# Routed experts of a decoder block: a third buffer of output rows, rows gathered four blocks ahead, and the down products of small blocks in four parts

## The chip, the core and the metric

The kernel runs on one core of a Trainium2 chip. The metric is device time in microseconds (us), from the first to the last instruction with the launch around it; smaller is better. The core has five engines that run their own instruction streams and wait for each other by semaphores: TensorE (PE in the profile, PEld for its weight loads), VectorE (DVE), ScalarE (ACT), GpSimd (POOL) and SyncE (SP). Sixteen DMA engines move data between the large memory (HBM) and the on-chip memories; POOL and SP both issue transfers to them.

## What is computed

The kernel is one layer of a decoder: a mixing part (a state-space branch and a sparse attention branch) and a channel part, a mixture of 64 experts for 1024 tokens of width 1024. Only the end of the channel part is touched. Cut to that, the reference is:

```
scores = sigmoid(xt @ w_router)                    # 1024 tokens x 64 experts
top_e  = the 8 best experts of each token (limited to 4 of 8 groups)
w      = scores[top_e] / sum * 2.5
# tokens sorted by expert, padded to blocks; for each block of one expert e:
rows = xt[tok]                                     # gather
hid  = silu(rows @ w_gate[e]) * (rows @ w_up[e])   # 1024 -> 256
out  = (hid @ w_down[e]) * wt[:, None]             # 256 -> 1024
routed = zeros.at[buf_tok].add(out)                # scatter with add
x = x + gate_f * (routed + shared)
```

All arithmetic is in float32. The output rows of a block are added to rows of the output that other blocks have added to as well, since a token has eight experts.

## The kernel before, in words

The mixing part, the router and the shared expert run first and take a little over half of the time; nothing in them changes. Then `moe()` (line 2099) walks the 64 experts, ordered by how many tokens they have. A planned number of slots for an expert (`QUOTA`, line 29) is cut into blocks of at most 128 slots: 32 experts have one block of 88 to 128 slots, the others a first block of 128 and then one or two blocks of 8 to 64. That makes 98 blocks: 64 of more than 64 slots, 16 of 48 or 64, and 18 of 8 to 32.

For block b the steps are: `gather(b)` (line 1853) fetches its token rows from HBM into one of three buffers `xg`, with an indirect DMA that POOL issues; `xpose(b)` (line 2131) transposes them on PE; `gu(b)` (line 2155) makes the gate and up products; `act(b)` the nonlinearity; `ht(b)` (line 2180) transposes the hidden rows; `dn(b)` (line 2200) makes the down products into a bank of PSUM, `o`; `put(b)` (line 2212) scales them into one of two buffers `ot` and issues the scatter with add to the output, again an indirect DMA from POOL. `put` writes `ot[b % 2]`, so it waits until the scatter of block b-2 has landed. All scatters write the same tensor, so the scatter of block b waits for the landing of the scatter of block b-1 as well.

Blocks of at most 64 slots use the array in parts side by side: a weight load of 32 or 64 columns leaves room beside it, and matmuls whose outputs lie at other partitions of PSUM go there. `gu` does so in four parts (32 columns) or two (64). `dn` uses two parts for all of them, with 512 columns of `w_down` each, at partitions 0 and 64.

The order is written out by hand at lines 2234 to 2273. In turn b of the loop stand, in this order: `gu(b)`; `gather(b + 3)`; `put(b - 2)`; two thirds of the splits of the next expert's weights (`units`, an ACT cast at line 2090 and a DVE subtraction at line 2091, eight of each per expert); `ht(b - 1)`; `act(b)`; `xpose(b + 2)`; `dn(b - 1)`; the rest of the splits; after an expert's last block, the loads of the weights three experts on (`w_load`, SP, three transfers of 1 MB); and one or two steps of background work (`bg`): picking the last tokens of the long lists (lines 1868 and 1869), `merge` (line 1871), which turns the lists into the row numbers that the gathers use, and tables for experts with more tokens than slots. Before the first gather of an expert with a long list (block 7) all the steps up to `merge` must have been issued.

On POOL the instructions of the loop are therefore: gather, scatter, gather, scatter, and so on, each in its turn.

Of the kernel before, what the change touches and what calls it, by code (L numbers as in the profile page):

```python
# [13 lines left out]
I32 = mybir.dt.int32  # L14
AF = mybir.ActivationFunctionType
OP = mybir.AluOpType
# [6 lines left out]
D = 1024  # L23
# [98 lines left out]
class Kernel:  # L122
# [1976 lines left out]
    def moe(self):  # L2099
        nc, I, fp, rp = self.nc, self.I, self.fp, self.rp  # L2100
        v = nc.vector
        mm = nc.tensor.matmul
        W, order = self.W, self.order
        r4 = self.r4
        r3, gates = self.r3, self.gt

        c = 3 * (D + 64)
        self.spare, self.nov = r3[:64, c:c + 640], r3[:1, c + 640:c + 641].bitcast(I32)
        hT = self.qp.tile([P, 2, 2, P], F32, name="hT", tag="qb")
        xhs = [self.qp.tile([P, 4, 280], F32R, name="xh", tag="wraw", bufs=2) for _ in range(2)]  # L2110
        xhs = [x.rearrange("p k n -> p (k n)")[:, :D].rearrange("p (k n) -> p k n", k=KT) for x in xhs]
        ots = [r4[:, i * D:(i + 1) * D] for i in range(2)]
        self.keysF = r4[:64, 2 * D:3 * D]

        xss = [r4[:, 2 * D + 512 * i:2 * D + 512 * i + 512] for i in range(2)]
        nc.gpsimd.memset(r4[:, 2 * D:3 * D], 0.0)
        hids = self.hids = [r4[:, 3 * D + 256 * i:3 * D + 256 * i + 256] for i in range(2)]
        self.ov = r4[:1, 3 * D + 512:4 * D].bitcast(I32)
        wts, self.cols = [gates[:, i:i + 1] for i in range(6)], gates[:64, 8:24]
        gf = self.gf = self.r_gf  # L2120
        depth, nr = sum(QUOTA[0]), [sum(len(x) > q for x in QUOTA) for q in range(3)]
        r0, _ = self.first_ranks()
        bg = self.take(self.taken, depth) + [lambda: self.merge(depth, [(0, 0, r0), (1, 0, nr[1]), (2, 0, nr[2])])]
        tables = self.overflow_tables()
        bg, left = bg + tables, len(tables)
        blocks, B = self.blocks, self.B
        nb = len(blocks)
        def units(e):
            return [lambda k=k: self.gu_part(e, k, v) for k in range(len(W[e]["gu"]), KT)]
# [70 lines left out]
        def dn(b):  # L2200

            s = B[b]
            n, w, st = s["n"], W[s["e"]]["dn"], s["hst"]
            if n > 64:
                s["o"] = [self.ps("o", "mm")[:n] for _ in range(2)]
            else:
                ps = self.ps("o", "mm")
                s["o"] = [ps[:n], ps[64:64 + n]]
            for k, h in [(k, h) for h in range(2) for k in range(2)] if n > 64 else [(k, h) for k in range(2) for h in range(2)]:
                mm(s["o"][h], st[:, k], w[:, k, 512 * h:512 * h + 512], start=k == 0, stop=k == 1)  # L2210

        def put(b):
            s = B.pop(b)
            n = s["n"]
            ot = ots[b % 2][:n]
            for h in (1, 0):
                c = slice(512 * h, 512 * h + 512)
                o = s["o"][h]
                if n <= 64 and h == 1:
                    o = ot[:, c]  # L2220
                    nc.scalar.copy(o, s["o"][1])
                v.scalar_tensor_tensor(ot[:, c], o, s["w"], gf[:n, c], op0=OP.mult, op1=OP.mult)  # L2222
            nc.gpsimd.indirect_dma_start(out=self.out, out_offset=bass.IndirectOffsetOnAxis(ap=s["ix"], axis=0),  # L2223
                                         in_=ot, in_offset=None, compute_op=OP.add)
# [2 lines left out]
        xpose(0)  # L2227
        for f in units(0):
            f()
        xpose(1)  # L2230
        for f in self.w_load(2, nc.sync):
            f()
        queue = []
        for b in range(nb + 2):
            if b < nb:
                e, r, q, n, first, last = blocks[b]
                if first:
                    assert not queue
                    if e + 1 < ne:
                        queue = units(e + 1)  # L2240
                    turns = len(QUOTA[r]) if e + 1 < ne else 1
                gu(b)
            if b + 3 < nb:
                while blocks[b + 3][1] < r0 and len(bg) > left:
                    bg.pop(0)()
                self.gather(b + 3)
            if 0 <= b - 2:
                put(b - 2)
            if b < nb:
                take = -(-len(queue) // max(turns, 1))  # L2250
                na = (take * 2 + 2) // 3
                for _ in range(na):
                    queue.pop(0)()
                if b > 0:
                    ht(b - 1)
                act(b)
                if b + 2 < nb:
                    xpose(b + 2)
                if b > 0:
                    dn(b - 1)  # L2260
                for _ in range(take - na):
                    queue.pop(0)()
                turns -= 1
                if last:
                    if e + 3 < ne:
                        for f in self.w_load(e + 3, nc.sync):
                            f()
                for _ in range(2 if 0 < b < self.rate[0] else b < self.rate[1] or b % 2):
                    if bg:
                        bg.pop(0)()  # L2270
            elif b == nb:
                ht(b - 1)
                dn(b - 1)
# [165 lines left out]
```

## Time and profile before

| | us |
|---|---|
| median of 3 runs | 2050.76 (2043.1 to 2051.07) |
| the profiled execution | 2056.37 |
| its span, first to last instruction | 2054.6 |
| PE busy in the span | 1910.8 (93%) |
| DVE busy | 1278.2 (62%) |
| ACT busy | 874.7 (43%) |
| POOL busy | 677.2 (33%) |

The span is 1.8 us shorter than the profiled execution, which is the launch around it; the profiled execution is 5.6 us above the median of the runs. Terms are worked out against the profiled execution. A wait in the profile is put down to what ended last by its records. Where the engine that it names had long been done, it was another, often a DMA.

### The profile page before, as it was taken

Reading aid. Unit: us, or ns where it says so; the run is one execution under the profiler, and the core shown is the slowest. Engines: PE = TensorE matmul, PEld = TensorE weight load, DVE = VectorE, ACT = ScalarE, POOL = GpSimd, SP = SyncE. Lnnn points to the kernel's source line nnn. Section 1 sums busy time; section 2 is a strip of 40 time slices with the busy share of each in tenths; the row PEclk is TensorE's granted clock in tenths of the full one; section 3 lists DMA queues with packets and bytes.
Section 4 is the critical chain, followed back from the end, with each engine's and each line's share of the span. In section 5 each row is a group of like instructions: output and inputs, shape, how many; then the busy total and the mean of one; then the engine's idle time right before and its main releaser. Section 6 shows DMA issues by size and latency. Waiting matters only on the chain. (4 is left out here: it accounts for less than half of the span.)

```text
span 2054.6 us, 31808 instructions
## 1 busy us (share of the span) xinstructions
PE 1910.8 (93%) x11227; PEld 1381.7 (67%) x11227; DVE 1278.2 (62%) x2875; ACT 874.7 (43%) x2113; POOL 677.2 (33%) x706
## 2 busy tenths in 40 slices
PE   5997999999899999999898999999999999999897
PEld 4785887889866655688776565666666666666563
DVE  5740694256778886557778765656665655656454
ACT  5221224125667666333334444444444444444332
POOL 7524231222032111234436334433332323323231
PEclk9998999999979999999999999999999999999998
DMA  8327430731023210464349998898989989989984
GB/s 289 92 83 89 106 101 26 239 96 42 22 83 104 71 53 21 151 214 154 134 144 250 367 294 303 270 300 304 299 288 313 300 290 294 308 291 311 278 233 110
DMA packets 150420, 396.31 MB, mean 193 GB/s; under 512 B 22049, under 2 KB 89298, under 8 KB 125666
## 3 DMA queue, kind: packets, MB, share of 16 engines
q1 hardware_dynamic: 117330, 288.28, 40.1%
q0 software_dynamic: 25152, 87.10, 18.8%
q10 hardware_dynamic: 7776, 18.88, 2.5%
q8 instruction: 89, 1.46, 0.3%
q14 instruction: 73, 0.60, 0.1%
HBM read 328.27 MB, written 64.23 MB: 191 GB/s over the span
## 5 line engine op out<-in xcount | busy, mean ns | idle before, releaser
L289 POOL TENSOR_TENSOR wlo<-wraw,whi 128x256 fp32r<-128x256 f32 (+1 forms) x238 | 198.2, 854 | 435.8 <-ACT whi L288 428.1
L2091 DVE TENSOR_TENSOR gl<-raw,gh 128x512 fp32r<-128x512 f32 x508 | 325.4, 688 | 22.5 <-ACT gh L2090 22.2
L2210 PE MATMUL o<-rawdn,hT 128*128 128x512 f32 (+10 forms) x784 | 312.2, 628 | 4.6 <-ACT hT L2189 4.5
L2090 ACT CAST gh<-raw 128x512 fp32r<-128x512 f32 x512 | 280.8, 628 | 13.2 <-DMA raw<-in_w_gu 13.2
L2223 POOL DMA_INDIRECT out<-ot,idx x64 | 115.6, 1806 | 368.1 <-DMA out<-ot,idx 122.0
L253 PE MATMUL gu<-gh,xh 128*128 128x512 f32 (+5 forms) x512 | 220.1, 430 | 0.0
L2222 DVE SCALAR_TENSOR_TENSOR ot<-o,wts,r_gf 128x512 f32<-128x512 f32 (+11 forms) x162 | 115.0, 742 | 152.8 <-DMA out<-ot,idx 66.2
L254 PE MATMUL gu<-gl,xh 128*128 128x512 f32 (+5 forms) x512 | 202.5, 395 | 0.0
L255 PE MATMUL gu<-gh,xl 128*128 128x512 f32 (+5 forms) x512 | 202.3, 395 | 0.0
L2210 PEld LDWEIGHTS o<-rawdn,hT 128*128 128x128 f32 (+10 forms) x784 | 105.5, 164 | 132.5 <-issue 118.8
L255 PE MATMUL mm<-hT_hi,wlo 128*128 128x512 f32 x352 | 141.0, 401 | 18.1 <-POOL wlo L289 18.1
L288 ACT CAST whi<-wraw 128x256 fp32r<-128x256 f32 (+1 forms) x264 | 95.8, 405 | 138.4 <-DMA wraw<-in_w_in 44.4
L253 PE MATMUL mm<-hT_hi,whi 128*128 128x512 f32 x352 | 142.1, 404 | 0.3 <-ACT hT_hi L467 0.3
L254 PE MATMUL mm<-hT_lo,whi 128*128 128x512 f32 x352 | 140.1, 398 | 0.2 <-DVE hT_lo L474 0.2
L253 PEld LDWEIGHTS gu<-gh,xh 128*128 128x128 f32 (+5 forms) x512 | 93.0, 182 | 56.5 <-issue 33.1
L2223 POOL DMA_INDIRECT out<-ot,back x34 | 57.9, 1704 | 215.7 <-DMA out<-ot,idx 160.7
L254 PEld LDWEIGHTS gu<-gl,xh 128*128 128x128 f32 (+5 forms) x512 | 93.0, 182 | 31.9 <-issue 7.9
L255 PEld LDWEIGHTS gu<-gh,xl 128*128 128x128 f32 (+5 forms) x512 | 92.6, 181 | 27.0
L2169 PE MATMUL gu<-raw,ot 128*32 128x128 f32 (+1 forms) x1664 | 100.2, 312 | 0.0
L1332 POOL TENSOR_TENSOR p<-p,ms 128x384 f32<-128x384 f32 (+7 forms) x52 | 45.7, 895 | 165.2 <-DVE ms L1325 86.7
L1318 ACT ACTIVATE p<-p,ms 128x384 f32<-128x384 f32 (+7 forms) x128 | 85.9, 673 | 32.6 <-DVE ms L1312 32.2
L2189 ACT COPY hT<-ht 128x256 f32<-128x256 f32 (+5 forms) x64 | 22.8, 356 | 180.5 <-PE ht L2188 180.0
(580 smaller groups left out, 4166.4 us busy)
## 6 DMA issues: line engine op xcount, KB each, us to landing
raw<-in_w_gu SPq DMA_DIRECT2D x124, 1024.0 KB, 10.1
rawdn<-in_w_down SPq DMA_DIRECT2D x62, 1024.0 KB, 11.2
wraw<-in_w_ada SPq DMA_DIRECT2D x32, 512.0 KB, 3.7
wraw<-in_w_in SPq DMA_DIRECT2D x28, 512.0 KB, 4.3
ada<-in_w_ada SPq DMA_DIRECT2D x16, 512.0 KB, 8.5
d_th<-th ACTq DMA_DIRECT2D x32, 256.0 KB, 2.0
wraw<-in_w_out SPq DMA_DIRECT2D x16, 512.0 KB, 4.6
x<-in_x SPq DMA_DIRECT2D x8, 512.0 KB, 6.4
```

The source lines that it names most:

```text
L253: mm(ps, lh, rh, start=start, stop=False)
L254: mm(ps, lh, rl, start=False, stop=False)
L255: mm(ps, ll, rh, start=False, stop=stop)
L288: self.nc.scalar.copy(hi, raw)
L289: (eng or self.nc.gpsimd).tensor_tensor(lo, raw, hi.bitcast(F32), op=OP.subtract)
L1318: nc.scalar.activation(p, p, AF.Exp, scale=-1.0, bias=m[:, nch - 1, h:h + 1], accum_out=m[:, 3, h:h + 1])
L2090: self.nc.scalar.copy(hi, src)
L2091: eng.tensor_tensor(lo, src, hi.bitcast(F32), op=OP.subtract)
L2169: mm(ps[m * j:m * j + m, :2 * c].rearrange("p (s n) -> p s n", s=2), s["st"][k], w["raw"][k][:, :, a:min(a + 2 * c, 256):2], start=k == 0, ...
L2210: mm(s["o"][h], st[:, k], w[:, k, 512 * h:512 * h + 512], start=k == 0, stop=k == 1)
L2222: v.scalar_tensor_tensor(ot[:, c], o, s["w"], gf[:n, c], op0=OP.mult, op1=OP.mult)
L2223: nc.gpsimd.indirect_dma_start(out=self.out, out_offset=bass.IndirectOffsetOnAxis(ap=s["ix"], axis=0), in_=ot, in_offset=None, compute_op= ...
```

## The change

`ots` gets a third slice, so that `put(b)` writes `ot[b % 3]`. Its room comes from the table `ov`, which moves to the tile `keys`, free by then. `gather` is issued one turn earlier: `gather(3)` ahead of the loop, and `gather(b + 4)` in turn b. The `xg` buffers stay three, so `gather(b + 4)` overwrites the rows of block b+1, which `xpose` has read in turn b-1; `merge` is due one turn earlier too, in turn 3.

For blocks of at most 32 slots `dn` uses four parts of 32 columns with 256 columns of `w_down` each. The weight load is always 32 columns, so `hT` is cleared once. `put` then takes four copies on ACT, one for each part, and one multiplication on DVE over 1024 columns, where there were one ACT copy of 512 and two DVE multiplications of 512.

```diff
+        nc.gpsimd.memset(hT, 0.0)
...
-        ots = [r4[:, i * D:(i + 1) * D] for i in range(2)]
+        ots = [r4[:, c:c + D] for c in (0, D, 3 * D + 512)]
...
-        self.ov = r4[:1, 3 * D + 512:4 * D].bitcast(I32)
+        self.ov = self.keys[:1].bitcast(I32)
...
+            if n <= 32:
+                ps = s["o"] = self.ps("o", "mm")
+                st = hT[:, b % 2, :, :32]
+                for k in range(2):
+                    for j in range(4):
+                        mm(ps[32 * j:32 * j + 32, :256], st[:, k], w[:, k, 256 * j:256 * j + 256], start=k == 0, stop=k == 1)
+                return
...
-            ot = ots[b % 2][:n]
-            for h in (1, 0):
+            ot = ots[b % 3][:n]
+            if n <= 32:
+                for j in range(4):
+                    nc.scalar.copy(ot[:, 256 * j:256 * j + 256], s["o"][32 * j:32 * j + n, :256])
+                v.scalar_tensor_tensor(ot, ot, s["w"], gf[:n], op0=OP.mult, op1=OP.mult)
+            for h in (1, 0) if n > 32 else ():
...
+        self.gather(3)
...
-            if b + 3 < nb:
-                while blocks[b + 3][1] < r0 and len(bg) > left:
+            if b + 4 < nb:
+                while blocks[b + 4][1] < r0 and len(bg) > left:
                     bg.pop(0)()
-                self.gather(b + 3)
+                self.gather(b + 4)
```

Three places of the program show what moves, on POOL, DVE and PE. The first is POOL at the start of the loop, from the gathers of blocks 4 and 5 on; "DMA xg" is a gather, "DMA out" a scatter, a DMASW semaphore tells that a transfer issued by POOL has landed, and the number of rows is in the shape of a gather. Before:

```order
L1858 DMA xg_10903<-d_h_65,idx_67 96x1088 [waits DVE_49,PE_49] x2
L2223 DMA out<-ot_11151,idx_67 1024x1024 [waits DMASW2_49,DMASW3_49,DMASW1_49,DVE_49]
L1858 DMA xg_10903<-d_h_65,idx_67 96x1088 [waits DMASW4_49,PE_49]
L2223 DMA out<-ot_11151,idx_67 1024x1024 [waits DMASW7_49,DVE_49]
L1858 DMA xg_10903<-d_h_65,idx_67 128x1088 [waits DMASW5_49,DVE_49,PE_49]
L2223 DMA out<-ot_11151,idx_67 1024x1024 [waits DMASW1_49,DVE_49]
```

and now:

```order
L1858 DMA xg_10903<-d_h_65,idx_67 96x1088 [waits DVE_49,PE_49] x2
L1858 DMA xg_10903<-d_h_65,idx_67 96x1088 [waits DMASW4_49,DVE_49,PE_49]
L2236 DMA out<-ot_11151,idx_67 1024x1024 [waits DMASW2_49,DMASW3_49,DMASW1_49,DVE_49]
L1858 DMA xg_10903<-d_h_65,idx_67 128x1088 [waits DMASW5_49,DVE_49,PE_49]
L2236 DMA out<-ot_11151,idx_67 1024x1024 [waits DMASW0_49,DVE_49]
```

The gather of the first block of 128 rows (block 7) now stands ahead of the second scatter instead of the third. The alternation is as it was, and each scatter after the first still waits for one earlier transfer (the scatter ahead of it) and for DVE.

The second is DVE at `merge` (lines 1876 to 1898), in turn 4 before and in turn 3 now. L2222 and L2235 are the multiplications of `put`, L1868 and L1869 the picks. Before:

```order
L2222 SCALAR_TENSOR_TENSOR ot_11151<-o,wts,r_gf 96x512 x2
L2091 TENSOR_TENSOR gl_10334<-raw,gh_10333 128x512 x6
L2178 TENSOR_TENSOR ot_11151<-ot_11151,gu 96x256
L2135 COPY wts<-xg_10903 96x1
L2153 TENSOR_TENSOR xl<-xt,xh 128x4x96 x2
L2091 TENSOR_TENSOR gl_10334<-raw,gh_10333 128x512 x2
L1868 MAX ot_11151<-keys 128x8
L1869 MATCH_REPLACE keys<-ot_11151,keys 128x272
L1868 MAX ot_11151<-keys 128x8
L1869 MATCH_REPLACE keys<-ot_11151,keys 128x264
L1876 COPY back<-ot_11151 64x312
```

and now:

```order
L1869 MATCH_REPLACE keys<-ot_11151,keys 128x264
L1876 COPY back<-ot_11151 64x312
L1894 TENSOR_TENSOR wts<-wts,tk 128x54
L1897 TENSOR_SCALAR idx_67<-wts 128x54
L1898 SCALAR_TENSOR_TENSOR idx_67<-idx_67,wts 128x54
L1894 TENSOR_TENSOR wts<-wts,tk 64x32
L1897 TENSOR_SCALAR back<-wts 64x32
L1898 SCALAR_TENSOR_TENSOR back<-back,wts 64x32
L1894 TENSOR_TENSOR wts<-wts,tk 64x2
L1897 TENSOR_SCALAR back<-wts 64x2
L1898 SCALAR_TENSOR_TENSOR back<-back,wts 64x2
L2235 SCALAR_TENSOR_TENSOR ot_11151<-o,wts,r_gf 96x512 x2
```

In both listings the first multiplications are `put(1)`: they stood ahead of the last picks and of `merge`, and now they stand behind them.

The third is PE at the first block of 8 slots: the end of the next block's gate and up products (gu), the hidden rows' transpose (ht), a later block's row transposes (xt), the down products (o). Before:

```order
L254 MATMUL gu<-gl_10334,xh 104x512
L255 MATMUL gu<-gh_10333,xl 104x512
L2191 MATMUL ht<-ident,ot_11151 64x128
L2141 MATMUL xt<-ident,xg_10903 128x8 x8
L2210 MATMUL o<-rawdn,hT 8x512 x4
```

and now:

```order
L254 MATMUL gu<-gl_10334,xh 104x512
L255 MATMUL gu<-gh_10333,xl 104x512
L2193 MATMUL ht<-ident,ot_11151 64x128
L2143 MATMUL xt<-ident,xg_10903 128x8 x8
L2211 MATMUL o<-rawdn,hT 32x256 x8
```

Four matmuls of 512 columns become eight of 256, at the same place.

## Rows read from the trace of the kernel before

**Rows 1.** Windows: length, busy time (count) of PE, PEld, DVE, ACT, POOL; clock, DMA share, GB/s

```profile
1218.00:2029.00 811.00, 774.08 (x4437) 497.07 (x4434) 486.92 (x892) 362.96 (x799) 270.74 (x173) 0.98 0.90 288
2029.00:2054.60 25.60, 11.61 (x37) 5.45 (x35) 3.23 (x5) 0.89 (x3) 4.77 (x3) 0.79 0.29 43
```

**Rows 2.** Line 2223, the scatters: ns min/median/max, first and last start; issue to landing

```profile
L2223 POOL DMA_INDIRECT out<-ot,idx x64: 1464/1598/4688, 1132.3 to 2046.0; - x64
...
DMA to landing us min/median/max: 3.1/8.4/12.1
```

**Rows 3.** Waits of POOL from 1218 to 2029: waiting <- ended by: us, times, longest

```profile
POOL out L2223 <- DMA out<-ot,idx: 275.5, 41, 9.8
POOL out L2223 <- DMA out<-ot,back: 88.0, 17, 7.8
POOL out L2223 <- DVE gl L2091: 51.0, 11, 9.7
```

**Rows 4.** Waits of PE in the same stretch

```profile
PE xt L2150 <- DMA xg<-d_h,idx: 22.4, 17, 3.2
PE xt L2141 <- DMA xg<-d_h,back: 11.6, 7, 4.0
```

**Rows 5.** Timeline near 1503: start, us, instruction, idle before it and what ended that

```profile
1502.79 1.41 DVE L2222 SCALAR_TENSOR_TENSOR ot<-o,wts,r_gf 112x512 f32<-112x512 f32 x2 [2.26 <-DMA out<-ot,idx]
...
1503.53 3.75 POOL L2223 DMA_INDIRECT out<-ot,back  x1 [5.99 <-DMA out<-ot,idx]
```

**Rows 6.** Timeline of POOL, 1590 to 1660, scatters alone ("back": not an expert's first block)

```profile
1592.55 1.62 POOL L2223 DMA_INDIRECT out<-ot,idx  x1 [6.01 <-DMA out<-ot,idx]
...
1605.19 1.34 POOL L2223 DMA_INDIRECT out<-ot,back  x1 [9.28 <-DMA out<-ot,idx]
...
1613.75 1.59 POOL L2223 DMA_INDIRECT out<-ot,idx  x1 [5.75 <-DMA out<-ot,back]
...
1620.89 1.39 POOL L2223 DMA_INDIRECT out<-ot,back  x1 [3.70 <-DMA out<-ot,idx]
...
1650.66 1.38 POOL L2223 DMA_INDIRECT out<-ot,back  x1 [7.79 <-DMA out<-ot,idx]
...
1655.41 1.62 POOL L2223 DMA_INDIRECT out<-ot,idx  x1 [1.90 <-DVE wts L2135]
```

**Rows 7.** Timeline of SP's queue there: issues of weight loads, 1 MB each

```profile
1592.12 1.50 SPq L2068 DMA_DIRECT2D raw<-in_w_gu  x2
...
1595.57 2.51 SPq L2068 DMA_DIRECT2D raw<-in_w_gu  x2
...
1621.87 1.24 SPq L2068 DMA_DIRECT2D raw<-in_w_gu  x2
```

**Rows 8.** Timeline of POOL at the end of the loop, its last three scatters

```profile
2029.12 1.61 POOL L2223 DMA_INDIRECT out<-ot,idx  x1 [4.79 <-DVE ot L2222]
2038.95 1.59 POOL L2223 DMA_INDIRECT out<-ot,idx  x1 [8.22 <-DVE ot L2222]
2046.05 1.57 POOL L2223 DMA_INDIRECT out<-ot,idx  x1 [5.51 <-DVEq L1964]
```

**Rows 9.** Timeline of POOL at the start of the loop, around `merge`

```profile
1143.84 2.77 POOL L2223 DMA_INDIRECT out<-ot,idx  x1 [8.19 <-DVE gl L2091]
1161.79 0.99 POOL L1858 DMA_INDIRECT xg<-d_h,idx  x1 [15.18 <-issue]
1164.93 4.69 POOL L2223 DMA_INDIRECT out<-ot,idx  x1 [2.15 <-DVE ot L2222]
```

**Rows 10.** Timeline of PE: down products of 8 slots, gate and up products of 8 slots

```profile
1320.23 1.89 PE L2210 MATMUL o<-rawdn,hT 128*8 128x512 f32 x8
...
1332.29 2.06 PE L2169 MATMUL gu<-raw,ot 128*32 128x128 f32 x64
```

**Rows 11.** Groups by shape, ACT copies out of PSUM: xcount | busy us, mean ns | idle before

```profile
L2189 ACT COPY hT<-ht 128x256 f32<-128x256 f32 x38 | 14.1, 372 | 114.3 <-PE ht L2188 113.9
...
L2221 ACT COPY ot<-o 8x512 f32<-8x512 f32 x5 | 2.9, 578 | 13.6 <-PE ht L2188 6.5 <-DMA out<-ot,idx 5.3 <-PE o L2210 1.7
```

## Prediction, before the changed kernel ran

> **What bounds the kernel now.** I began with the windows of the expert loop [rows 1]. Between 1218 and 2029 us PE is busy for 774.08 of 811.00 us, and 34.0 us of its idle time is one wait, for gathered rows to land [rows 4]. Read alone, that says that PE is the bound and that earlier gathers would help. So I looked for what makes a gather late. It stands on POOL behind a scatter, and POOL's waits in this stretch [rows 3] are nearly all one kind: 58 scatters waited 363.5 us for an earlier scatter to land, and 30 more are put down to engines, of which the group put down to line 2091 (51.0 us, 11 times) is the largest. Line 2091 writes nothing that a scatter reads, so there the DMA is the likelier cause.
>
> The sizes confirm it. 88 scatters start between 1218.21 us and the start at 2029.12 us [rows 8], about 810.9 us, or 9.21 us each. A scatter takes 8.4 us (median) from issue to landing [rows 2]. The next starts some 0.7 us later: near 1503 one landing releases a DVE multiplication at 1502.79 and the next scatter at 1503.53 [rows 5]; with the release itself I take 0.8. 88 x (8.4 + 0.8) = 810 us. **So the scatters are a serial chain without a gap, as long as the loop.** All wait for their predecessor because they add to the same output. PE, with 774 us of work beside 811, is second; its 34 us of waiting is handed down: chain, POOL's place in line, gather, PE. In the same way the two `ot` buffers make DVE wait for the landing that the next scatter waits for too [rows 5].
>
> **The change part by part.**
>
> *Third buffer.* It lets `put(b)` run once the scatter of block b-3 has landed. It does not let a scatter start earlier, since each still waits for its predecessor; POOL's new order shows that wait. DVE, ACT and PE may stand one block further ahead of the chain. They do so once, and then wait for it again. Inside the stretch: 0 us.
>
> It pays where the chain has gaps because the data come late. At the end it has one. The last scatters start at 2029.12, 2038.95 and 2046.05 [rows 8]. These blocks are alike (88 slots), and the last spacing, 7.10 us, is that of a scatter that waited for its predecessor. The one before could have started at 2029.12 + 7.10 = 2036.2, and started at 2038.95, when its multiplication was done: a gap of 2.7 us. With PE one block ahead it closes: **-2.7 us**; bounds 0 and -2.7 here. Next late is the chain itself.
>
> *Gathers one turn earlier.* A gather's place on POOL stays between the same kinds of scatters; it fetches one block further on. The 34.0 us of PE's waits [rows 4] may go, but PE then reaches the third buffer's limit and waits there. Credited: 0 us. The gather now overwrites rows that `xpose` read one turn later than before, which adds a wait for PE and DVE on POOL, with the next scatter queued behind it. But that transpose stands in turn b-1 ahead of `put(b-2)`, whose scatter is the one queued: that scatter needs later work anyhow. 0 us. The DMAs that the gathers issue are the same, and no other POOL work lies in the loop.
>
> *`merge` one turn earlier.* Before, the gather of block 7 waited 15.18 us for its row numbers and issued at 1161.79; the third scatter followed at 1164.93, 21.1 us after the second at 1143.84 [rows 9]. Now that wait falls before the second scatter. A turn lasts some 9 us (the chain's spacing), so `merge` should end at about 1152 to 1153 and the second scatter start there instead of at 1143.84; the third follows after a landing near a load, up to 12.1 us [rows 2], at 1163 to 1165, where it is now. Taken: 0; bounds -2 and +9 (all the delay of the second scatter passed on).
>
> *Down products in four parts.* The trace has no four-part down product, but it has one in two parts, 1.89 us, and a four-part `gu`, 64 instructions of 128 columns in 2.06 us [rows 10]. A float32 matmul is two instructions there. The new form is 16 instructions of 256 columns, half the columns of that `gu`: 1.03 us. The saving is 0.86 us for each of 18 blocks, 15.5 us of PE. If parts did not run side by side here, it would be about four times 1.03, +2.2 us each, +40 us of PE, and 774 + 40 would pass the chain by 3. PE is not the bound, so credited: 0, between +3 and -15.5.
>
> *Its `put`.* One ACT copy of 512 columns takes 578 ns; one of 256 columns takes 372 ns [rows 11], so four take 1.49 us, +0.91 us, 16 us in all on an ACT that is busy for 363 of 811 us [rows 1]. DVE has one instruction fewer for the same columns. The put ends about 0.9 us later, hidden as its scatter waits for its predecessor (POOL sat idle for 9.28 us before the small one at 1605.19 and 3.70 before that at 1620.89 [rows 6]). Taken: 0; bounds 0 and +16. Clearing `hT` is one POOL instruction of 512 columns before the loop: 0.
>
> The Trainium skill (TensorEngine Tiling (Array Packing), PSUM Bottleneck) speaks against this part: tiling speeds up TensorE but not the evacuation of PSUM, which may become the bottleneck. If so here, the sum would carry the +16; the ACT rows agree that evacuation grows, and the idle time says that it is covered.
>
> *Sum.* 2056.4 - 2.7 = 2053.7 us for an execution like the profiled one. That one lies 5.6 us above the median, so against the runs: 2048; I take 2047, as the chain's first gaps may close a little too.
>
> **The rivals.**
>
> *PE is the bound after all.* Then its 34.0 us and the 15.5 us go: 2047 - 49.5 = 1998 us. For: PE is 95% busy. Against: the chain's own sum. It needs landings that are short by themselves and only look long.
> The Trainium skill (DMA: Bandwidth & Descriptors, Anatomy of one DMA — SWDGE (gpsimd) path) prices a DMA from POOL at about 2.0 us plus bytes over 436e3 per us; for 128 rows of 4 KB that is an estimate of 3.2 us, and by it no chain would bind and this rival would win. The trace disagrees here: 8.4 us median, 12.1 at most [rows 2].
>
> *The weight loads meet the chain better.* A landing depends on what else the DMA engines carry. From 1592 two experts' weights are issued [rows 7]; the scatter of a 128-slot block issued then holds the chain for 12.64 us (1592.55 to 1605.19), while one at 1613.75, with the loads mostly in, holds it for 7.14 [rows 6]. For a small block it is 8.56 us (from 1605.19) against 4.75 (from 1650.66). A load that meets a large block costs 5.5 us, a small one 3.8: 1.7 us between. PE one block further ahead moves every load by a block against the chain. There are some 30 such pairs of loads; if ten move from large to small blocks, 17 us go: 2030 us. DMA share is already 0.90, which caps this.
>
> *They meet it worse.* The same mechanism with the other sign: in turns where the load is issued, it falls on the 128-slot scatter instead of the small one behind it. Ten pairs: +17, 2064 us; from six pairs on (10 us) it is slower than the bound below. Nothing in the rows tells the sign; the order of large and small experts is mixed, so most should cancel.
>
> *Evacuation binds.* ACT's 16 us on the path: 2063 us. It needs the 18 puts to end after their predecessor's landing, against the idle time above.
>
> *The change does not do what it says* (the parts don't run side by side): +3 at most, inside the forecast.
>
> **How the numbers follow.** Measurement can tell about 0.5%, 10 us, from no change. Forecast (chain holds, 2041 to 2059: -2 and +9 of `merge`, +3 of the down product, and the 4 us by which the runs before spread to either side): 0.60. Better meeting: 0.20. PE the bound: 0.07. Worse meeting: 0.09. Evacuation: 0.04. So faster by over 0.5%: 0.27; within: 0.60; slower: 0.13. The predicted time is that of the likeliest case, 2047. The range reaches from the better meeting to the forecast's upper end, with 2 us to spare at either: 2028 to 2061; 2064, 2063 and 1998 are left out, 0.20.
>
> **What would show it.** In the profile after: scatters still start some 0.8 us after the landing before them, POOL's largest waits are for scatters, the sum over the stretch stays near 811 us; PE's waits for gathered rows shrink while DVE's waits for landings, or PE's for DVE, take their place; the down product of small blocks takes about 1.0 us; the gap before the last scatter but one is gone; the third scatter starts near 1165. The forecast is wrong if the median landing moves by over 0.1 us (88 x 0.1 = 9 us), or if scatters start well after their predecessor's landing.

## The result, and the profile after

The changed kernel takes 2027.36 us (median of 4 runs, 2020.39 to 2029.22) where the kernel before takes 2049.44; the ratio is 0.9886, with a 95% interval of 0.9861 to 0.991. That is 22 us, and 0.6 us below the range of the prediction. Two later measurements of the same kernel gave 0.9911 (0.9888 to 0.9933) and 0.9905 (0.9871 to 0.994), so about 20 us is the better figure. A profile is one run: the one before took 2056.4 us, 7 above the median, the one after 2029.2, so the two traces lie 27 us apart, and differences between them are somewhat larger than those of the medians.

The windows of the changed kernel's loop, to set beside [rows 1]; columns are length, busy time (count) of PE, PEld, DVE, ACT, POOL, then clock, DMA share, GB/s:

```profile
1216.00:2004.60 788.60, 758.35 (x4597) 502.34 (x4593) 486.46 (x875) 377.54 (x854) 253.30 (x173) 0.99 0.92 296
2004.60:2027.30 22.70, 3.81 (x10) 1.17 (x8) 2.80 (x4) 0.30 (x1) 4.73 (x3) 0.64 0.33 49
```

The scatters, at line 2236 now, to set beside [rows 2]; nanoseconds min/median/max of the instruction, then issue to landing:

```profile
L2236 POOL DMA_INDIRECT out<-ot,idx x64: 1484/1602/4701, 1128.5 to 2018.7; - x64
...
DMA to landing us min/median/max: 3.3/7.8/12.2
```

The loop is 22 us shorter, and the median landing fell from 8.4 to 7.8 us. I added up the landings one by one (issue to landing of the scatters numbered 8 to 93, counted from 0, in both traces): 718.1 us before, 696.6 after, 21.5 less. What lies between a landing and the next scatter stayed: 73.3 us before, 73.7 after. So the scatters are still one chain without a gap. Its links got shorter, and the prediction had held them fixed.

Waits by engine: PE's largest in the stretch from 1216 to 2004, then SP's three largest, for the weight loads (line 2068: gate and up; line 2078: down), after, and SP's two largest before, from 1218 to 2029. Columns are waiting, what ended it, us, times, longest; [rows 4] are PE's before:

```profile
PE xt L2152 <- DMA xg<-d_h,idx: 27.9, 13, 5.1
```

```profile
SPq L2068 <- PE gu L2171: 413.9, 57, 20.4
SPq L2078 <- PE o L2211: 98.2, 13, 7.9
SPq L2078 <- PE o L2219: 77.5, 9, 8.8
```

```profile
SPq L2068 <- PE gu L2169: 412.4, 55, 20.1
SPq L2078 <- PE o L2210: 204.0, 22, 13.4
```

The third fence is what the prediction should have read: in the trace of the kernel before SP waits for hardly anything but PE. A load goes out when PE has used the old weights. Whatever moves PE against the chain of scatters moves the loads against it.

By how much can be counted. For each of the 186 weight loads of the loop I took the scatter number at its issue (scatters started by then, with the fraction of the way to the next). Over loads 15 to 185 the changed kernel issues a load **0.69 scatters earlier** than the kernel before, some 6 us.

What that does is seen near the loads of one expert. Before, the scatter of a two-block expert's first block of 128, the one of its small second block, the one of a one-block expert; then SP's loads in the same stretch:

```profile
1747.22 1.61 POOL L2223 DMA_INDIRECT out<-ot,idx  x1 [8.11 <-DMA out<-ot,idx]
1756.15 1.38 POOL L2223 DMA_INDIRECT out<-ot,back  x1 [4.92 <-DMA out<-ot,idx]
1764.41 1.64 POOL L2223 DMA_INDIRECT out<-ot,idx  x1 [5.48 <-DMA out<-ot,back]
1773.80 1.60 POOL L2223 DMA_INDIRECT out<-ot,idx  x1 [6.47 <-DMA out<-ot,idx]
```

```profile
1756.96 2.14 SPq L2068 DMA_DIRECT2D raw<-in_w_gu  x2
1760.41 0.35 SPq L2078 DMA_DIRECT2D rawdn<-in_w_down  x1
```

The same blocks after:

```profile
1734.92 1.60 POOL L2236 DMA_INDIRECT out<-ot,idx  x1 [8.10 <-DVE gl L2091]
1742.10 1.80 POOL L2236 DMA_INDIRECT out<-ot,back  x1 [4.28 <-DMA out<-ot,idx]
1751.23 1.64 POOL L2236 DMA_INDIRECT out<-ot,idx  x1 [6.05 <-DVE wts L2137]
1758.53 1.58 POOL L2236 DMA_INDIRECT out<-ot,idx  x1 [4.41 <-DVE wts L2137]
```

```profile
1737.45 2.14 SPq L2068 DMA_DIRECT2D raw<-in_w_gu  x2
1740.71 0.35 SPq L2078 DMA_DIRECT2D rawdn<-in_w_down  x1
```

Before, the load starts after the small scatter has (1756.96 against 1756.15) and is still running under the next big one, which holds the chain for 9.39 us. After, it starts 2.5 us into the big scatter that precedes the small one, and that scatter still takes 7.18 us. The small one lies under the load (9.13 us against 8.26), and the next big one is nearly free of it: 7.30 us. The three together take 23.61 instead of 26.58 us. The loads are not all that moved here: behind these three scatters POOL issues the gathers of blocks of 64, 128 and 128 slots before, and of 128, 128 and 64 slots after.

Over the whole loop, from scatter 8 to scatter 93, the windows before and after:

```profile
1231.20:2016.70 785.50, 749.03 (x4307) 482.14 (x4301) 469.95 (x864) 351.08 (x774) 261.49 (x169) 0.98 0.91 292
1228.90:1993.90 765.00, 735.20 (x4448) 487.45 (x4448) 475.86 (x857) 370.13 (x836) 245.09 (x169) 0.99 0.93 299
```

785.50 x 0.91 = 715 us of DMA work before, 765.00 x 0.93 = 711 after: the same. What fell is the engines' idle time, 71 to 53 us (summed from the packets), and it fell in one place: between the start of a scatter of 64 slots or fewer and the next scatter, from 30.7 us to 7.7. Under the big ones it went from 40.5 to 45.4. A small scatter has few packets of its own (8 slots are eight packets, of 0.33 us each for four of the five such scatters before, and the shortest landing is 3.1 us [rows 2]), so the engines are idle there unless another transfer runs, and a transfer that runs there costs the chain less than one under a big scatter (the prediction's rows give 3.8 and 5.5 us for a load).

What fills that time now is not more weights. Summed from the packets, weights took 167 us of the engines' time at the small scatters before and 161 after; gathered rows took 22 us before and 44 after, and at the big scatters 71 and 51. The gather that POOL issues right behind a scatter used to belong to the block six further on and now belongs to the seventh, and big and small blocks take turns: of some 7620 rows gathered in the loop, 2768 were issued behind a small scatter before, and 3920 are now. **So the transfers meet the chain better**, as in the rival "the weight loads meet the chain better", and with the time that it gave, 2030 us; but the gathered rows, which it leaves out, moved too.

### The profile page after: what moved, and what is told of

Read it like the earlier page. It is cut to its first block, busy times and chain, and to the rows that moved or that the text cites. A ratio compares the mean times of both kernels' runs of the same rounds, so it can differ in the third digit from the quotient of the medians.

```text
span 2027.3 us, 32106 instructions
## 1 busy us (share of the span) xinstructions
PE 1884.4 (93%) x11359; PEld 1381.1 (68%) x11371; DVE 1274.5 (63%) x2857; ACT 888.3 (44%) x2167; POOL 660.4 (33%) x707
## 4 chain that ended last, share of the span: by engine, by line
PE 28%; DMA 16%; DVE 4%; issue 3%; POOL 2%; ACT 1%; POOLq 0%; SPq 0%; ACTq 0%; DVEq 0%
PE o L2219 8%; DMA out<-ot,idx 6%; DMA xg<-d_h,idx 6%; PE gu L253 3%; PE gu L254 3%; PE gu L255 3%; PE gu L2171 3%; DMA out<-ot,back 2%; PE xt L2152 2%; DMA out<-y 1%; PE xt L2143 1%; POOL out L2236 1%; DMA raw<-in_w_gu 1%; PE mm L253 1%; PE mm L254 1%
## 5 line engine op out<-in xcount | busy, mean ns | idle before, releaser
L2219 PE MATMUL o<-rawdn,hT 128*128 128x512 f32 (+7 forms) x640 | 267.7, 607 | 6.8 <-ACT hT L2191 6.7
L2219 PEld LDWEIGHTS o<-rawdn,hT 128*128 128x128 f32 (+7 forms) x640 | 97.5, 175 | 117.7 <-issue 102.6
L2235 DVE SCALAR_TENSOR_TENSOR ot<-o,wts,r_gf 128x512 f32<-128x512 f32 (+7 forms) x144 | 101.8, 744 | 119.6 <-PE o L2219 63.4
L2236 POOL DMA_INDIRECT out<-ot,back x34 | 50.5, 1484 | 220.7 <-DMA out<-ot,idx 125.7
L254 PEld LDWEIGHTS gu<-gl,xh 128*128 128x128 f32 (+5 forms) x512 | 92.4, 180 | 31.4 <-issue 7.9
L2180 DVE TENSOR_TENSOR ot<-ot,gu 128x256 f32<-128x256 f32 (+7 forms) x98 | 35.1, 358 | 117.2 <-ACT ot L2179 113.0
L2152 PE MATMUL xt<-ident,xg 128*128 128x128 f32 (+5 forms) x512 | 72.3, 288 | 30.7 <-DMA xg<-d_h,idx 29.7
L1318 ACT ACTIVATE p<-p,ms 128x384 f32<-128x384 f32 (+7 forms) x128 | 85.9, 673 | 32.6 <-DVE ms L1312 32.2
```

Of the source, the lines that this page charges most:

```text
L254: mm(ps, lh, rl, start=False, stop=False)
L1318: nc.scalar.activation(p, p, AF.Exp, scale=-1.0, bias=m[:, nch - 1, h:h + 1], accum_out=m[:, 3, h:h + 1])
L2152: nc.tensor.transpose(ps[:, k], x[:, 4 * q + k:D:KT], self.ident[:n, :n])
```

## Experiments

Each ratio is to the kernel before on the same chip.

### Which part: one at a time, and two together

Third buffer and gathers, without the four-part product:

```diff
-        ots = [r4[:, i * D:(i + 1) * D] for i in range(2)]
+        ots = [r4[:, c:c + D] for c in (0, D, 3 * D + 512)]
...
-            ot = ots[b % 2][:n]
+            ot = ots[b % 3][:n]
...
-                self.gather(b + 3)
+                self.gather(b + 4)
```

> Third buffer of output rows and gathers four blocks ahead; down products and put as before. Lead theory (the scatters remain one chain; PE, DVE and ACT stand one block further ahead of it, so weight loads are issued earlier against the chain, the DMA engines idle less and landings get shorter): nearly all of the gain is here, ratio to before 0.985 to 0.991, about 2020 to 2031 us, sum of the landings of the loop near 713 as in the full change. PE-time theory (the four-part product frees PE and with it the weight buffers sooner): little is left, ratio 0.996 to 1.0, sum of landings near 735 as before. Chance-phase theory (where loads meet scatters is luck): anything between 0.985 and 1.01.

Measured: 0.9936 (0.9913 to 0.9959), 2037.6 us, between the ranges of the lead theory and the PE-time theory: some 13 of the 20 us. The sum of landings in the profiled run is 697.7 us, as in the full change (that run lies 11 us under its kernel's median), the loads' shift 0.63 scatters earlier.

The four-part product alone (the edits of `dn` and `put` in the change):

> Down products and put of blocks of up to 32 slots in four parts; two buffers and gathers three ahead as before. Lead theory: PE's 15 us go into waiting, ratio 0.997 to 1.003. PE-time theory: most of the gain, ratio 0.985 to 0.992. Evacuation rival: 1.005 or more. In every theory the small product takes about 1.0 us instead of 1.89.

Measured: 1.0006 (0.9987 to 1.0025); the loads do not move (0.05 scatters later).

The third buffer alone (`ots` and `b % 3`, gathers three ahead):

> Third buffer of output rows alone. Lead theory, with the buffer as the limit of the lead: half of the gain or more, ratio 0.987 to 0.995, and DVE's waits for landings in its multiplication fall from 105 us to about 50. If the gathers are the limit: PE keeps waiting 34 us for rows, ratio 0.997 to 1.0. PE-time theory: 1.0. The gap before the last scatter but one (2.7 us) closes in any case if the buffer is what closed it.

Measured: 1.0014 (0.9988 to 1.004); no move of the loads (0.07 later). DVE's waits for landings are gone; what is left of its waits at line 2223, us, times, longest:

```profile
DVE ot L2223 <- PE o L2211: 79.2, 53, 3.8
DVE ot L2223 <- ACT ot L2222: 21.3, 27, 2.2
```

PE still waits for gathered rows:

```profile
PE xt L2151 <- DMA xg<-d_h,idx: 22.1, 17, 3.4
PE xt L2142 <- DMA xg<-d_h,back: 19.6, 6, 4.8
```

The gathers four ahead alone (`b + 4`, two buffers):

> Gathers four blocks ahead alone. Lead theory, buffer as the limit: ratio 0.998 to 1.003, since the block with the rows at hand still waits for one of two output buffers. Gathers as the limit: 0.988 to 0.994 and PE's 34 us of waits for rows gone. The second scatter moves from 1144 to about 1152 in any case.

Measured: 0.9985 (0.9966 to 1.0004); the loads go out 0.15 scatters earlier. It is the mirror image of the buffer alone: PE waits for no rows at all, but for ACT, which stands behind the landing that DVE waits for:

```profile
PE o L2211 <- ACT hT L2190: 32.1, 16, 5.7
```

```profile
DVE ot L2223 <- DMA out<-ot,idx: 69.2, 20, 6.6
DVE ot L2223 <- DMA out<-ot,back: 62.2, 17, 6.3
```

So PE's lead over the chain has two limits, the rows and the output buffer, and they stood at about the same place. Lifting one leaves the other; lifting both moves PE, and with it the loads. Neither theory about a single part stands. "The buffer is the limit" would have given half of the gain or more, and the gathers alone would have given 0.988 to 0.994 if they had been the limit.

### Is the chain the bound

The changed kernel with every other scatter of the loop going to a scratch tensor, so that these rows are missing from the output:

```diff
-            nc.gpsimd.indirect_dma_start(out=self.out, ...
+            nc.gpsimd.indirect_dma_start(out=self.d_alt if 8 <= b < 92 and b % 2 else self.out, ...
```

> The changed kernel with the scatters of every other block of the loop (odd blocks 9 to 91) added to a scratch tensor of the same size, so that these rows are missing from the output; bytes and counts are the same, but a scatter waits only for the scatter two blocks before it. If the serial chain is what holds the loop: ratio 0.970 to 0.980 to before (PE, busy 758 of 789 us, or the DMA engines, busy 712 of 765, become the bound), 1990 to 2010 us. If the DMA engines or PE are already the bound: 0.985 to 0.99, within 8 us of the changed kernel.

Measured: 0.9703 (0.9673 to 0.9733), 1986.9 us, 40 below the changed kernel. The window 1230 to 1950 of that kernel:

```profile
1230.00:1950.00 720.00, 716.96 (x4447) 478.54 (x4436) 470.09 (x849) 362.84 (x828) 269.49 (x169) 1.00 0.99 318
```

PE is idle for 3 of 720 us, and the DMA engines are full as well. The chain was the bound, and the next two bounds stand 40 us behind it, side by side. The median landing is 10.6 us here and costs nothing, as two are in flight.

The same with the two-part product back:

```diff
-            if n <= 32:
-                ps = s["o"] = self.ps("o", "mm")
...
-            for h in (1, 0) if n > 32 else ():
+            for h in (1, 0):
```

> The kernel with two chains of scatters (odd blocks 9 to 91 added to a scratch tensor, so missing from the output) with the down product and put of small blocks back in two parts. If PE is the bound once the chain is out of the way, the 15.5 us that the four parts save show now: 1987 + 15 = 2002 us, ratio 0.975 to 0.979. If the DMA engines are the bound there: within 4 us of 1987.

Measured: 0.9756 (0.9728 to 0.9783), 1998.5 us. The four parts are worth some 0.5%, 11 us (the two intervals just touch), once PE is the bound, of the 15.5 us of PE that they save; 0 when the chain is (1.0006).

A third of the weight bytes left out, so that the products use old weights:

```diff
-            for h in range(2):
+            for h in range(2 if e < 3 else 1):
                 c = slice(2048 * h, 2048 * h + 2048)
```

> The changed kernel without the second half of each gate and up load from expert 3 on (2 MB of 3 MB per expert are fetched; the products use stale weights). If landings are long because weights are in flight: median landing of the loop from 7.8 to about 6.5 us, the chain falls below PE's 758 us and PE binds, 1985 to 2000 us. If landings are long by themselves: 7.8 us and 2027 us stay.

Measured: 0.9685 (0.9659 to 0.9712), 1986.3 us. The scatters of that kernel, and its window:

```profile
DMA to landing us min/median/max: 3.3/6.8/12.8
```

```profile
1230.00:1950.00 720.00, 715.25 (x4457) 478.52 (x4451) 468.34 (x847) 361.38 (x824) 249.33 (x168) 1.00 0.83 242
```

The median landing falls from 7.8 to 6.8 us, and PE binds. Landings are longer when more weights are in flight.

### Do the loads do it by themselves

First try: all loads held back by one turn.

```diff
+                if late is not None:
+                    nc.sync.dma_start(self.d_tick[b:b + 1], hids[b % 2][:1, :8])
+                    for f in self.w_load(late, nc.sync):
+                        f()
...
+                if last and e + 3 < ne:
+                    late = e + 3
```

> The changed kernel with the weight loads of an expert held back on SP by one turn: a 32-byte store of the next block's hidden row stands ahead of them, so SP waits for that block's activation. Meeting theory (the gain comes from weight loads that are issued 0.7 scatters earlier against the chain, and so run under the scatters of small blocks, whose time leaves the DMA engines idle): the shift is undone, ratio to before 0.998 to 1.02, idle DMA time in the loop back from 53 to 70 us or more. PE theory (the gain is PE and the DVE work around it being free of waits): 0.986 to 0.991, as the changed kernel, as long as PE waits for no weights.

Measured: 1.0188 (1.013 to 1.0246). It settles nothing, since the loads came 2 scatters later than in the changed kernel and something new waits for them:

```profile
ACT gh L2090 <- DMA raw<-in_w_gu: 199.7, 72, 8.6
```

Second try: the down load ahead of the gate and up load of the same expert.

```diff
-        return [gu, dn]
+        return [gu, dn] if e < 3 else [dn, gu]
```

> The changed kernel with the load of w_down issued ahead of that of w_gu of the same expert, from expert 3 on. The down load waits for a down product late in the turn, so bursts of two experts' weights (5 MB within 4 us, every 27 us) break into two of 3 MB, and all loads come up to 8 us later. Meeting theory: which scatters lie under loads changes; if evenness counts, idle DMA time falls below 53 us and the ratio to before is 0.975 to 0.985; if earliness counts, 0.99 to 1.0. PE theory: no change, 0.986 to 0.991.

Measured: 1.0084 (1.0063 to 1.0106), outside every range of the expectation: 36 us above the changed kernel on the same chip, with no engine waiting for weights. In the profiled run 12 us of the loss stand before scatter 8 and 20 in the loop, whose 786 us are those of the kernel before again. So the PE theory is out. But earliness by itself isn't what counts: on average the loads still go out 0.47 scatters earlier than in the kernel before. The ones that a one-block expert frees are back where they stood before (0.07 scatters later, from block 11 on), the others come 0.79 earlier. And the order of the loads changed here as well as their time.

Third try: only the loads that a one-block expert frees wait a little, for the transposed rows of the next block but one; and a control whose store waits for nothing (it reads `gf[:1, :8]`).

```diff
+                        if first and b > 10:
+                            t = B[b + 2]["st"][KT - 1]
+                            t = (t[1] if isinstance(t, tuple) else t)[:1, :8].bitcast(F32)
+                            nc.sync.dma_start(self.d_tick[b:b + 1], t)
                         for f in self.w_load(e + 3, nc.sync):
```

> The changed kernel with a 32-byte store on SP ahead of the loads that a one-block expert frees, which reads what the next-but-one block's transposed rows were copied to: the loads go out some 3 to 4 us later in the same turn, 0.35 scatters, half of the shift. Meeting theory: a part of the gain goes, in proportion half, ratio to before 0.993 to 1.000. If timing by a few us is not what counts: 0.988 to 0.992. ACT and PE should wait for no weights in either case.

> The same store in the same place, but it reads a constant row, so it waits for nothing: control for what the store itself costs on SP (0.4 us) and in the DMA engines. 0.988 to 0.992 in both theories.

Measured: later 0.9956 (0.9932 to 0.9981), control 0.9916 (0.9886 to 0.9946). These intervals overlap at their ends, but the two kernels ran on one chip and can be set against each other directly: the medians are 2040.0 (12 runs) and 2032.0 us (7 runs), the means lie 8.4 us apart, with a 95% interval of 2.9 to 14.0. The changed kernel on the same chip is at 2029.2. So the delay costs about half of the control's 17 us. The delay was larger than expected, since these loads used to follow the other expert's almost at once: 3.8 us behind them in the control (1609.28 to 1613.06), and 14.9 in the delayed kernel (1612.69 to 1627.57). SP's queue in the control, then in the delayed kernel:

```profile
1609.28 1.24 SPq L2068 DMA_DIRECT2D raw<-in_w_gu  x2
1611.30 0.34 SPq L2078 DMA_DIRECT2D rawdn<-in_w_down  x1
1611.69 0.34 SPq L2282 DMA_DIRECT2D d_tick<-r_gf  x1
1613.06 1.27 SPq L2068 DMA_DIRECT2D raw<-in_w_gu  x2
```

```profile
1612.69 1.24 SPq L2068 DMA_DIRECT2D raw<-in_w_gu  x2
1615.54 0.34 SPq L2078 DMA_DIRECT2D rawdn<-in_w_down  x1
...
1625.92 0.29 SPq L2283 DMA_DIRECT2D d_tick<-ot  x1
1627.57 1.29 SPq L2068 DMA_DIRECT2D raw<-in_w_gu  x2
```

Against the control these loads go out 0.72 scatters later, the others 0.15 earlier; against the kernel before 0.10 later and 0.76 earlier, nearly the places of the down-first kernel. Buffers, gathers and products are those of the changed kernel, and nothing waits for weights. The loop, from scatter 8 to 93, in the delayed kernel and in the control:

```profile
1231.30:2016.10 784.80, 744.68 (x4449) 491.78 (x4450) 475.02 (x857) 370.77 (x836) 250.82 (x169) 0.97 0.92 292
```

```profile
1229.70:1989.60 759.90, 734.77 (x4447) 487.39 (x4446) 476.23 (x857) 370.14 (x836) 236.60 (x169) 0.98 0.94 301
```

These two profiled runs lie 26 us apart where the medians lie 8: the one of the delayed kernel is 12 us above its median, the one of the control 7 under. In that run the loop is as long as before the change, though the third buffer and the early gathers are there.

All the one-chain kernels without a wait for weights, by their profiled runs. "At small scatters" is the time from the start of a scatter of up to 64 slots to the next scatter; there stand the engines' time on weights, on gathered rows, and their idle time, each averaged over the 16 engines:

| kernel | loop, scatter 8 to 93, us | weights at small scatters, us | gathered rows at small scatters, us | idle at small scatters, us |
|---|---|---|---|---|
| changed (three profiles) | 765, 767, 755 | 161, 162, 173 | 44, 44, 42 | 7.7, 8.2, 3.8 |
| buffer and gathers (two) | 765, 766 | 171, 176 | 44, 42 | 8.8, 8.7 |
| control | 760 | 173 | 43 | 6.5 |
| gathers alone | 776 | 182 | 29 | 21.6 |
| four parts alone | 781 | 145 | 19 | 32.5 |
| delayed loads | 785 | 125 | 31 | 26.3 |
| before | 786 | 167 | 22 | 30.7 |
| down first | 786 | 140 | 35 | 26.2 |
| buffer alone | 792 | 150 | 25 | 34.6 |

The twelve profiles fall in two groups without an overlap: with up to 8.8 us of idle time at the small scatters the loop takes 755 to 767 us, with 21.6 and more 776 to 792 (the profile of the gathers alone lies 9 us under its kernel's median). The DMA work of the loop is 706 to 725 us; the delayed loads and down first are at the upper end (725 and 724, the control 711), so there over half of the longer loop is packets that take longer, not idle time.

So what counts is how the transfers fall among the scatters, and not PE's own time. That the place of the loads has an effect of its own is shown by the delayed loads against the control; down first points the same way, by more, but changes the order too. How much of the gain of the change is the loads, and how much the gathered rows, is not shown: no run moves the loads earlier with the gathers in their old places. The gathers alone, which do move to their new places, gain 0.15%, at most 0.34% or 7 us, with the loads 0.15 scatters earlier.

### Is the four-part product worth anything

> The changed kernel once more, for a ratio on the same chip as the others: 0.986 to 0.991 expected; with third buffer and gathers alone at 0.9936, the four-part product would be worth 0.3 to 0.7% once the lead is there, though it was worth nothing by itself (1.0006). If it comes out at 0.992 or more, the four-part product is worth nothing here either.

> The changed kernel, beside the next one on the same chip: 0.987 to 0.992.

> Third buffer and gathers without the four-part product. If the four parts are worth something once the lead is there: 0.3 to 0.6% above the changed kernel. If PE is not the bound, as the gap of 40 us to the version with two chains says: within 0.2%.

Measured: changed kernel 0.9911 (0.9888 to 0.9933) and 0.9905 (0.9871 to 0.994), without the four parts 0.9944 (0.992 to 0.9968) and, above, 0.9936. The ratios' intervals overlap in each pair, but the second pair ran on one chip: the means lie 9.1 us apart there, with a 95% interval of 2.6 to 15.6 (medians 2029.2 and 2037.9). So it is worth some 0.4% on top of the other two, and nothing alone. How is open: the loads' shift (0.63 to 0.69 against 0.61 to 0.63) hardly differs. That the earlier end of a small down product frees the down weights earlier is only a guess.

### A version that beats both

The two chains, with everything computed: the shared expert's rows are stored to a second tensor instead of being added to the output, odd blocks are added to that tensor, and it is added to the output near the end.

```diff
-                        nc.gpsimd.dma_start(self.out[i * P:(i + 1) * P], ys[i], accum_op=OP.add)
+                        nc.gpsimd.dma_start(self.d_alt[i * P:(i + 1) * P], ys[i])
...
+            nc.gpsimd.indirect_dma_start(out=self.d_alt if b <= 91 and b % 2 else self.out, ...
+            if b == 91:
+                for i in range(KT):
+                    nc.gpsimd.dma_start(self.out[i * P:(i + 1) * P], self.d_alt[i * P:(i + 1) * P], accum_op=OP.add, max_dma_last_dim=4096)
```

> A candidate from the two chains that computes everything: the shared expert's rows are stored to a second tensor instead of added to the output, odd blocks up to 87 are added to that tensor, and after block 87 eight DMAs of 128 rows add it to the output; then one chain again. 1024 packets of 4 KB at 0.327 us on 16 engines are 21 us, some 24 with issue and landing, during which scatters wait; the last ten blocks win back part, as landings without loads take 4.5 to 6.3 us and PE needs about 9 us a block. Expected 1990 to 2002 us, ratio 0.971 to 0.977. If the joining is dearer than its packets say (DRAM to DRAM, both ways): up to 2015.

> The same, joined after block 91: four blocks less to win back the joining, 1994 to 2006 us; later than the version joined after block 87 by 2 to 8 us if the chain after the joining sets the end, equal if PE does.

Measured: joined after block 87 0.979 (0.9768 to 0.9812), 2005.7 us; after block 91 **0.9782** (0.9758 to 0.9805), 2004.3 us, 23 below the changed kernel's first median. POOL at the join, in the second:

```profile
1930.15 6.83 POOL L2240 DMA_DIRECT2D out<-d_alt  x8 [7.43 <-DMA d_alt<-ot,idx]
1961.51 1.62 POOL L2236 DMA_INDIRECT out<-ot,idx  x1 [24.53 <-DMA out<-d_alt]
```

The join takes 31.4 us instead of 24, and 39.7 in the first. The 24 left out the weights, which are still in flight in both: 3 MB, 8.5 us of the engines' time, in the second, and 6 MB, 15.5 us, in the first (summed from the packets). In the second the chain sets the end, as the expectation's first case has it: the scatters after the join each wait for the landing before them. But the first is not earlier by 2 to 8 us, and misses its 1990 to 2002 us: its join is longer, and PE waits there for rows whose gather stood behind the join:

```profile
PE xt L2143 <- DMA xg<-d_h,back: 18.6, 1, 18.6
```

## Why the prediction was wrong, step by step

- **The chain as the bound**: right. Scatters still follow a landing with the same gap (73.3 and 73.7 us in all), and with two chains the kernel takes 40 us less, and PE is the bound.
- **Third buffer, "inside the stretch: 0 us"**: the step that failed, with the line of gathers one turn earlier, which was also credited 0. The argument was that PE stands one block further ahead once and then waits for the chain again. That DVE's waits for landings would take the place of PE's waits did not come true (105.6 us of such waits before, 48.6 after). The chain's links are not fixed: the loads hang on PE, and 0.6 to 0.7 scatters more lead put them elsewhere among the scatters. Of the gathers the prediction said that their DMAs are the same. They are, but behind other scatters: 3920 rows instead of 2768 behind small ones. The two together measured 11 to 13 us (0.9944 and 0.9936), against 0, and 0 for each alone. I had looked for what the lead does to the waits and not for what it does to the transfers, though SP's waits for PE stood in the trace.
- **The gap at the end, -2.7 us**: the size was right and the cause wrong. The last three scatters of the changed kernel follow each other by 7.04 and 7.10 us, to set beside [rows 8]:

```profile
2004.55 1.61 POOL L2236 DMA_INDIRECT out<-ot,idx  x1 [4.02 <-DMA out<-ot,back]
2011.59 1.59 POOL L2236 DMA_INDIRECT out<-ot,idx  x1 [5.43 <-issue]
2018.69 1.59 POOL L2236 DMA_INDIRECT out<-ot,idx  x1 [5.52 <-DMA out<-ot,idx]
```

  But with the buffer alone the gap is still there (2031.53 to 2040.33), and with the gathers alone it is gone (2013.60 to 2020.64). What came late at the end was the rows.
- **`merge` one turn earlier, 0**: right to a few microseconds. The second scatter was forecast at 1152 to 1153 and the third at 1163 to 1165; to set beside [rows 9]:

```profile
1148.53 1.00 POOL L1858 DMA_INDIRECT xg<-d_h,idx  x1 [18.34 <-PE tk L1890]
1151.30 4.70 POOL L2236 DMA_INDIRECT out<-ot,idx  x1 [1.76 <-DVE ot L2235]
...
1162.78 2.35 POOL L2236 DMA_INDIRECT out<-ot,idx  x1 [4.85 <-DVE gl L2091]
```

- **Four parts, 1.03 us, and their `put`**: sizes right. An 8-slot product on PE, and the copies on ACT (ns min/median/max), to set beside [rows 10] and [rows 11]:

```profile
1309.26 1.07 PE L2211 MATMUL o<-rawdn,hT 128*32 128x256 f32 x16
```

```profile
L2227 ACT COPY ot<-o x72: 355/364/369, 1216.3 to 1620.4; 8x256 f32<-8x256 f32 x20, 16x256 f32<-16x256 f32 x20, 24x256 f32<-24x256 f32 x16, 32x256 f32<-32x256 f32 x16
```

  Credited 0, and 0 alone (1.0006); but on top of the other two they bring some 9 us, so here the credit of 0 failed as well, for a reason that stays open. The evacuation rival, which rested on the Trainium skill (TensorEngine Tiling (Array Packing), PSUM Bottleneck), doesn't show: the same run bounds it at 0.25%, 5 us, where it would have cost 16.
- **The rival that came true** had 0.20, which was too little, and half of its picture. Its price was of the right order (1.7 us for a pair of loads that moves from a big scatter to a small one; 26.58 to 23.61 us for three blocks in the stretch shown, where the gathers moved too). But I said that the rows don't tell the sign and that most should cancel. They didn't cancel: all six profiles with both the buffer and the gathers, and the loads in their new places, have the short loop. Nor was it weights in sum that went to the small scatters (167 us there before, 161 to 176 in these six), but gathered rows (22 before, 42 to 44). The Trainium skill (DMA: Bandwidth & Descriptors, Queues, rings and completion order) says that a DMA engine takes turns between the queues that have work, packet by packet. The traces agree on the turns: in the join after block 87, while weights are in flight too, each of the two has about half of the engines' time (0.51 and 0.52 from 1895 to 1920 us). How much goes in one turn no run here shows. The median landing of 7.8 us, 6.8 with a third of the weights left out, fits the turns.
- **PE the bound**: 1998 us forecast if the chain were no bound; with two chains PE is, at 1986.9.
- **The range**: the upper end of the forecast, 2059, leaves out the 4 us of spread that its own list names (2047 + 9 + 3 + 4 = 2063). The measured time lies at the other end.

## What to carry to other kernels

When an engine gets more room to run ahead, ask which transfers its progress releases, and where they then fall among the transfers on the critical path; a serial chain's step time is no constant while other queues share its DMA engines. Two limits that stand at the same place hide each other, so an edit that lifts one of them measures nothing, and only the pair says what either is worth. And where a serial chain of read-modify-write transfers is the bound, two chains into two tensors with a join at the end may be worth more than any shortening of the compute beside it (2004 against 2027 us here).

## What the hardware showed that I had not expected

- The DMA work of the loop varies by 19 us over twelve profiles (706 to 725 us), its time by 37 (755 to 792): the rest is what the chain leaves idle.
- A scatter that adds to memory takes far longer than its packets: with no weights in flight the scatters of 88 slots at the end land in 6.2 to 6.3 us, where 88 packets of 0.328 us on 16 engines are 1.8, and in the loop with two chains the median is 10.6.
- Adding one 4 MB tensor in memory to another with eight DMAs took 31.4 us from the first issue to the next scatter with 3 MB of weights beside it and 39.7 with 6 MB, against 21 us by its packets alone (1024 of 0.327 us on 16 engines). In the second case a gather issued behind it landed with it, 32.6 us after its issue.
